# Where the first operand and seven weight blocks of the second output stage are prepared in a two-layer hybrid encoder kernel

## Chip, cores and metric

One core of one Trainium2 chip runs the whole program. The metric is the device time in microseconds (us) of one execution; for the kernel before it is the median of three runs.

## What is computed

The reference runs two layers over 2048 tokens of width 1024. Layer 0 has windowed attention, layer 1 dense latent attention with 16 heads; each is followed by the same kind of output stage. What matters here is layer 1:

```python
logits = (einsum('bqhd,bshd->bhqs', qn_b, k_nope) + einsum('bqhr,bsr->bhqs', qr_b, k_rope)) * scale
probs = softmax(logits, axis=-1)
o = einsum('bhqs,bshd->bqhd', probs, v)          # dense attention, 16 heads
y = (o * silu(z)) @ w_out                        # output stage, first product
h = h + y
gate = sigmoid(rms_norm(h, ple_norm_g) @ ple_w_gate)
h = h + (p @ ple_w) * gate
out = rms_norm(h, final_norm_g)
```

## The kernel before, in words

Every 32-bit factor is split into a high part (a cast to the fp32r type) and a low part (the difference), and a product is three matmuls (`mm3`, L290 to L292). The split of a block in SBUF is `split_sbuf`: ACT casts the high part (L216), and POOL or DVE subtracts (L218).

The program is a list of steps, each with a due time; `Plan.run` sorts them and writes the instructions of PE, ACT, DVE and POOL in that order, and each engine works its own list in order. The order of the DMA issues on SP is left to the scheduler. Due times in the dense attention count steps; in the output stages a time in us is multiplied by `US` = 1/1.3 to become steps.

**Dense attention** (`Dense`): 64 units (16 heads x 4 groups of 512 queries) of 16 steps, one step for 128 keys. A step `kt` of unit `u` issues on PE three score products (L1622 to L1624), one product of a coming unit whose row maximum is wanted (L1591, `max_step`), and two value products (L1654, L1655), which run 4.3 steps later. ACT does the exponential (L1626) and the cast to the high part (L1627). POOL subtracts for the low part (L1634). DVE reduces the maximum product (L1595, called the reduction below) and adds the probabilities to their sum in PSUM (L1644, the sum). The maximum products write to two PSUM banks in turn (`m_ps`), so one of them waits until the reduction of the one two before it is done. Once a unit, two products for the denominators (L1681, at 8.4 steps) and a transpose (L1607, at 9.6) take a turn in these same two banks, DVE splits the finished sum (L223), adds the two halves of the output (L1663) and folds the maxima (L1600). The maximum products run one to two units ahead, so the last 24 steps (from step 8 of unit 62) have none, and no reductions.

**Output stage** (`Post`, the second object, `final`): for the first 512 tokens `o_load` fetches a block of the attention output, its reciprocal denominators and its gate, `o_gate` multiplies them in two instructions (L768 and L769), and `o_cut` splits the result into the operand (L216, L218). Eight such blocks make the first operand. `w_load` and `w_split` do the same for a 1024 x 128 block of the weights (L703; L216 and L218 on 128x1024). `front` is one product of 24 matmuls over the eight operand blocks and one weight block. The operands of later token groups go through L757 (PE), L764 (DVE), L765 (POOL), L216 and L218.

`enter` turns the tables of `early_tables` into steps: a `w` entry is the due time of a split, with its load 4 us ahead; an `o` entry is the due time of the products, the distance to the split, the block, and which engines multiply. "dve" puts both products on DVE; "both" puts the first on POOL and the second on DVE. Times count from the start of the output stage, half a step after the end of the dense attention.

Of the kernel before, what the change touches and what calls it, by code (L numbers as in the profile page):

```python
# [73 lines left out]
GATES = [45, 55, 65, 126] + [(25 + i) * UNIT + 1 for i in range(4)]  # L74
E_W, E_O, E_P, E_M = (-16.54, -8.54, -0.54), -44.33, 4.77, ('mix', 'mix', 'mix', 'mix', 'mix', 'mix', 'mix', 'mix')
def early_tables():
    return (
    {
        "w": ([E_W[0], E_W[1], E_W[2], 5, 11, 17, 21, 25], GATES),
        "o": [(E_O + E_P * i, 2.5, i, E_M[i]) for i in range(8)],  # L80
        "renew": [(0.2, (("X", F32R), ("Y", F32R)))],
    },
    {
        "w": ([-4, 1, 5, 9, 13, 17, 21, 25], GATES),
        "o": [(-31 + 3.6 * i, 1.2, i, "dve") for i in range(8)],
        "renew": [(32 * UNIT + 1, (("Z", F32),))],
    },
)
# [1665 lines left out]
@with_exitstack  # L1754
def trunk(ctx, tc: tile.TileContext, a: dict, out):
    k = K(tc.nc, tc, a, ctx)
    rest = phase_a1(k)
    plan = Plan(k)
    end = phase_a2(k, plan, rest) + BASE[0]
    post = Post(k, 0, SPOTS[0], k.a_o, k.a_rden, k.a_z, a["a_w_out"][0], a["c_xT"], k.h1, 3)  # L1760
    end = post.enter(plan, end, early_tables()[0]) + BASE[1]
    end = Latents(k).schedule(plan, end) + BASE[2]
    dense = Dense(k)
    end = Gates(k).schedule(plan, end, dense) + BASE[3]
    end = dense.schedule(plan, end) + BASE[4]
    post = Post(k, 1, SPOTS[1], k.b_o, k.b_rden, k.b_z, a["b_w_out"][0], k.h1, out, 1)
    post.enter(plan, end, early_tables()[1])
    plan.run()
# [42 lines left out]
```

## Time and profile before

| | us |
|---|---|
| median of three runs | 3708.15 (3703.82 to 3709.5) |
| profiled execution | 3707.77 |
| its span in the trace | 3705.7 |
| PE busy | 3559.0 (96%) |
| DVE, ACT, POOL busy | 2400.5 (65%), 2277.3 (61%), 1969.9 (53%) |

A busy PE is not yet one at its own pace: matmuls overlap, and what counts is the distance from one start to the next. In the trace an engine's row tells start, duration, line, operation and tiles; a bracket at its end is the idle time ahead of it and what ended that. The stretches that matter are the dense attention (about 1760 to 3275 us of the span) and the first 100 us of the output stage behind it.

### The profile page before, as it was taken

The numbers are of one execution on the slowest core, as the hardware profiler recorded it, in microseconds if no ns is written. First come the engines' busy times: TensorE is split into PE (matmuls) and PEld (weight loads), VectorE is DVE, ScalarE is ACT, GpSimd is POOL, SyncE is SP. The second block draws the span as 40 slices with busy tenths as digits, with TensorE's granted clock in tenths as the row PEclk, the third lists the DMA queues.
The fourth block names the chain that finished last, engine by engine and source line by source line (L and its number), as shares of the span: only waits on it lengthen the run. The fifth ranks groups of instructions, "written<-read, shape, count | busy, mean of one in ns | idle before, by whom it ended". The sixth has DMA issues, their size and how long they took to land. (4 is left out here: it accounts for less than half of the span.)

```text
span 3705.7 us, 52399 instructions
## 1 busy us (share of the span) xinstructions
PE 3559.0 (96%) x17102; PEld 2971.5 (80%) x17102; DVE 2400.5 (65%) x4507; ACT 2277.3 (61%) x4267; POOL 1969.9 (53%) x1564
## 2 busy tenths in 40 slices
PE   6999999998999899999999999999999999989997
PEld 5788878886777799899888888888888888767776
DVE  5211149996444444523989898989898989964445
ACT  5211169995233443422989898989898989852333
POOL 3332120024324433110989898989898989953243
PEclk8999999999999999999999999999999999999998
DMA  6433278887754676654121212121212121166633
GB/s 169 129 119 111 75 204 203 200 193 204 168 151 131 175 203 204 220 190 136 26 58 35 58 35 58 35 58 36 56 35 55 38 63 35 31 192 170 172 98 106
DMA packets 384888, 429.25 MB, mean 116 GB/s; under 512 B 50579, under 2 KB 237459, under 8 KB 383910
## 3 DMA queue, kind: packets, MB, share of 16 engines
q1 hardware_dynamic: 365598, 391.81, 39.2%
q10 hardware_dynamic: 19016, 34.10, 2.6%
q8 instruction: 134, 2.20, 0.3%
q14 instruction: 140, 1.15, 0.1%
HBM read 252.71 MB, written 156.18 MB: 110 GB/s over the span
## 5 line engine op out<-in xcount | busy, mean ns | idle before, releaser
L1634 POOL TENSOR_TENSOR blkR<-blkF,blkX 128x512 fp32r<-128x512 f32 x1024 | 1351.0, 1331 | 180.3 <-PE ps L1624 51.3
L1595 DVE TENSOR_REDUCE blkF<-ps 128x1 f32<-128x512 f32 x1024 | 700.3, 684 | 79.2 <-PE ps L1591 43.8
L1626 ACT ACTIVATE blkF<-ps 128x512 f32<-128x512 f32 x1024 | 611.0, 597 | 101.1 <-PE ps L1624 60.8
L1627 ACT CAST blkX<-blkF 128x512 fp32r<-128x512 f32 x1024 | 635.4, 621 | 32.8
L1644 DVE TENSOR_TENSOR ps<-ps,blkF 128x512 f32<-128x512 f32 x896 | 615.4, 687 | 0.7
L1655 PE MATMUL ps<-blkR 128*128 128x512 f32 x1024 | 405.7, 396 | 1.1 <-POOL blkR L1634 1.1
L1654 PE MATMUL ps<-blkX,blkR 128*128 128x512 f32 x1024 | 405.7, 396 | 0.0
L290 PE MATMUL ps<-blkR 128*128 128x512 f32 (+2 forms) x888 | 342.9, 386 | 8.2 <-ACT blkR L216 8.2
L291 PE MATMUL ps<-blkR 128*128 128x512 f32 (+2 forms) x888 | 341.3, 384 | 1.2 <-DVE blkR L218 1.2
L292 PE MATMUL ps<-blkR 128*128 128x512 f32 (+2 forms) x888 | 340.9, 384 | 0.6 <-DVE blkR L218 0.6
L819 POOL TENSOR_TENSOR blkF<-blkF 128x512 f32<-128x512 f32 (+1 forms) x112 | 145.1, 1296 | 249.2 <-ACT blkF L813 239.1
L352 DVE TENSOR_TENSOR blkF<-ps,blkF 128x512 f32<-128x512 f32 x72 | 49.3, 691 | 329.8 <-PE ps L292 278.7
L218 POOL TENSOR_TENSOR blkR<-blkF,blkR 128x1024 fp32r<-128x1024 f32 (+1 forms) x39 | 73.4, 1885 | 306.1 <-ACT blkR L216 278.5
L1655 PEld LDWEIGHTS ps<-blkR 128*128 128x128 f32 x1024 | 195.0, 190 | 46.9 <-POOL blkR L1634 2.3
L1654 PEld LDWEIGHTS ps<-blkX,blkR 128*128 128x128 f32 x1024 | 195.0, 190 | 44.3
L813 ACT ACTIVATE blkF<-blkF 128x512 f32<-128x512 f32 (+1 forms) x120 | 72.2, 602 | 223.8 <-DVE blkF L798 114.4
L290 PEld LDWEIGHTS ps<-blkR 128*128 128x128 f32 x888 | 172.4, 194 | 40.5 <-ACT blkR L216 9.4
L292 PEld LDWEIGHTS ps<-blkR 128*128 128x128 f32 x888 | 171.6, 193 | 32.3 <-DVE blkR L218 1.2
L291 PEld LDWEIGHTS ps<-blkR 128*128 128x128 f32 x888 | 171.8, 193 | 31.1 <-DVE blkR L218 1.9
L223 DVE TENSOR_TENSOR blkR<-ps,blkR 128x512 fp32r<-128x512 f32 (+2 forms) x232 | 143.6, 625 | 52.3 <-ACT blkR L222 51.8
L290 PE MATMUL ps<-blkR,blkX 128*128 128x512 f32 (+1 forms) x384 | 150.4, 392 | 22.1 <-DVE blkF L352 13.8
L1622 PE MATMUL ps<-blkZ 96*128 96x512 f32 x384 | 155.6, 405 | 6.7 <-ACT blkF L1626 6.7
(268 smaller groups left out, 9021.2 us busy)
## 6 DMA issues: line engine op xcount, KB each, us to landing
h<-blkF SPq DMA_DIRECT2D x96, 256.0 KB
blkF<-h SPq DMA_DIRECT2D x80, 256.0 KB
a_qs<-blkF ACTq DMA_DIRECT2D x64, 256.0 KB
ple<-blkF SPq DMA_DIRECT2D x64, 256.0 KB
blkF<-h SPq DMA_DIRECT2D x32, 512.0 KB
b_v<-blkX SPq DMA_DIRECT2D x32, 512.0 KB
b_q<-blkX SPq DMA_DIRECT2D x64, 256.0 KB
blkZ<-b_q SPq DMA_DIRECT2D x64, 256.0 KB
```

What stands on the lines that cost most here:

```text
L290: mm(out, lhsT=lh, rhs=rh, start=(first and i == 0), stop=False)
L291: mm(out, lhsT=lh, rhs=rl, start=False, stop=False)
L292: mm(out, lhsT=ll, rhs=rh, start=False, stop=(last and i == n - 1))
L819: getattr(self.k.nc, eng).tensor_tensor(out=acc, in0=acc, in1=sq, op=ALU.add)
L1595: nc.vector.tensor_reduce(out=mm[:, qt, kc : kc + 1], in_=ps, axis=AX.X, op=ALU.max)
L1622: nc.tensor.matmul(sp, lhsT=kl[:, kt_], rhs=qh[0:96, :], start=True, stop=False)
L1626: nc.scalar.activation(pe, sp, AF.Exp, scale=SCALE_B)
L1627: nc.scalar.copy(ph, pe)
L1634: nc.gpsimd.tensor_tensor(out=pl, in0=pe, in1=fv(ph), op=ALU.subtract)
L1644: nc.vector.tensor_tensor(out=st["acc"], in0=prev, in1=st[kt][0], op=ALU.add)
L1654: nc.tensor.matmul(st["o"], lhsT=v, rhs=ph, start=(kt == 0), stop=False)
L1655: nc.tensor.matmul(st["o"], lhsT=v, rhs=pl, start=False, stop=(kt == NT - 1))
```

## The change

One table is changed, that of the second output stage. The eight operand blocks, prepared from 31 us ahead of the stage in distances of 3.6 us by DVE alone, are now due at -200, -181, -163, -145, -127, -110, -92 and -33 us, with the first product on POOL and the split 2.6 us behind the products instead of 1.2. Of the eight weight blocks, due from -4 to 25 us before, seven are now due at -190, -173, -153, -137, -68, -55 and -43 us, and the eighth at 13.

```diff
     {
-        "w": ([-4, 1, 5, 9, 13, 17, 21, 25], GATES),
-        "o": [(-31 + 3.6 * i, 1.2, i, "dve") for i in range(8)],
+        "w": ([-190, -173, -153, -137, -68, -55, -43, 13], GATES),
+        "o": [(t, 2.6, i, "both") for i, t in enumerate((-200, -181, -163, -145, -127, -110, -92, -33))],
         "renew": [(32 * UNIT + 1, (("Z", F32),))],
     },
```

In steps, operand blocks 0 to 7 come at unit 54 step 6, unit 55 step 5, unit 56 step 3, unit 57 steps 0 and 14, unit 58 step 11, unit 59 step 9 and unit 62 step 7. Weight blocks 0 to 6 come at unit 54 step 14, unit 55 step 11, unit 56 step 10, unit 57 step 7, unit 60 step 12 and unit 61 steps 6 and 15. The list of PE is the same in both kernels.

On DVE, in unit 54, the rows around steps 5 to 8 were these before (reduction and sum in turn, then the fold):

```order
L1644 TENSOR_TENSOR ps<-ps,blkF 128x512
L1595 TENSOR_REDUCE blkF<-ps 128x1
L1644 TENSOR_TENSOR ps<-ps,blkF 128x512
L1595 TENSOR_REDUCE blkF<-ps 128x1
L1644 TENSOR_TENSOR ps<-ps,blkF 128x512
L1600 TENSOR_REDUCE blkF<-blkF 128x4
```

and are these now:

```order
L1644 TENSOR_TENSOR ps<-ps,blkF 128x512
L769 TENSOR_TENSOR blkF<-blkF 128x512
L1595 TENSOR_REDUCE blkF<-ps 128x1
L1644 TENSOR_TENSOR ps<-ps,blkF 128x512
L1595 TENSOR_REDUCE blkF<-ps 128x1
L1644 TENSOR_TENSOR ps<-ps,blkF 128x512
L1600 TENSOR_REDUCE blkF<-blkF 128x4
L218 TENSOR_TENSOR blkR<-blkF,blkR 128x512
```

The second product of block 0 (L769) stands ahead of the reduction of step 7, and the subtraction of its split (L218) behind that of step 8.

On POOL, whose list holds the low parts of all 1024 steps (L1634), this stood from the start of the dense attention to that of the output stage:

```order
L1545 MEMSET blkR 1x2048
L1634 TENSOR_TENSOR blkR<-blkF,blkX 128x512 x1024
L731 TENSOR_TENSOR blkR<-ident 128x1024
L733 MEMSET blkR 128x512 x2
L819 TENSOR_TENSOR blkF<-blkF 128x512
```

and this stands there now, with the first products (L768) of the first three blocks:

```order
L1545 MEMSET blkR 1x2048
L1634 TENSOR_TENSOR blkR<-blkF,blkX 128x512 x871
L768 TENSOR_TENSOR blkF<-blkF 128x512
L1634 TENSOR_TENSOR blkR<-blkF,blkX 128x512 x14
L768 TENSOR_TENSOR blkF<-blkF 128x512
L1634 TENSOR_TENSOR blkR<-blkF,blkX 128x512 x14
L768 TENSOR_TENSOR blkF<-blkF 128x512
```

Eight products have come into POOL's list; the first stands behind the low part of step 6 of unit 54.

On DVE, in unit 62 behind the last reduction, this stood before, the first two of eight groups:

```order
L1600 TENSOR_REDUCE blkF<-blkF 128x4
L768 TENSOR_TENSOR blkF<-blkF 128x512
L769 TENSOR_TENSOR blkF<-blkF 128x512
L1644 TENSOR_TENSOR ps<-ps,blkF 128x512
L218 TENSOR_TENSOR blkR<-blkF,blkR 128x512
L1644 TENSOR_TENSOR ps<-ps,blkF 128x512 x2
L768 TENSOR_TENSOR blkF<-blkF 128x512
L769 TENSOR_TENSOR blkF<-blkF 128x512
```

and this stands there now, block 7 with it:

```order
L769 TENSOR_TENSOR blkF<-blkF 128x512
L1595 TENSOR_REDUCE blkF<-ps 128x1
L1644 TENSOR_TENSOR ps<-ps,blkF 128x512 x2
L1600 TENSOR_REDUCE blkF<-blkF 128x4
L218 TENSOR_TENSOR blkR<-blkF,blkR 128x512
L1644 TENSOR_TENSOR ps<-ps,blkF 128x512 x5
```

Seven of the eight groups have left the last 24 steps.

## Rows read from the trace of the kernel before

**Rows 1.** Busy time by stretch: us; PE, PEld, DVE, ACT, POOL (count); clock; DMA share, GB/s.

```profile
3080.00:3174.00 94.00, 94.00 (x407) 76.06 (x406) 85.77 (x145) 85.03 (x148) 85.95 (x67) 1.00 0.13 35
3174.00:3268.00 94.00, 88.27 (x362) 69.23 (x361) 87.61 (x130) 80.71 (x141) 82.73 (x60) 0.96 0.24 66
```

**Rows 2.** Timeline of PE, one steady unit: start, duration, line; step 7, step 8, denominators.

```profile
3093.04 0.40 PE L1591 MATMUL ps<-blkR,blkZ 96*128 96x512 f32 x1
...
3094.44 0.40 PE L1591 MATMUL ps<-blkR,blkZ 96*128 96x512 f32 x1
...
3095.13 0.62 PE L1681 MATMUL ps<-blkE,ones 128*128 128x512 f32 x2
```

**Rows 3.** Timeline of DVE in the same unit: reductions of steps 6, 7 and 9.

```profile
3092.64 0.68 DVE L1595 TENSOR_REDUCE blkF<-ps 128x1 f32<-128x512 f32 x1
...
3093.84 0.68 DVE L1595 TENSOR_REDUCE blkF<-ps 128x1 f32<-128x512 f32 x1
...
3096.72 0.69 DVE L1595 TENSOR_REDUCE blkF<-ps 128x1 f32<-128x512 f32 x1 [0.34 <-PE ps L1591]
```

**Rows 4.** Timeline of ACT in the same unit: the cast of step 6.

```profile
3092.52 0.62 ACT L1627 CAST blkX<-blkF 128x512 fp32r<-128x512 f32 x1
```

**Rows 5.** Timeline of POOL in the same unit: seven low parts, then that of step 9.

```profile
3087.84 9.45 POOL L1634 TENSOR_TENSOR blkR<-blkF,blkX 128x512 fp32r<-128x512 f32 x7 [0.34 <-PE ps L1591]
...
3097.86 1.30 POOL L1634 TENSOR_TENSOR blkR<-blkF,blkX 128x512 fp32r<-128x512 f32 x1 [0.56 <-ACT blkX L1627]
```

**Rows 6.** Line 769: instructions, duration in ns (min/median/max), first and last start.

```profile
L769 DVE TENSOR_TENSOR blkF<-blkF x8: 1635/1662/1673, 3234.4 to 3272.5; 128x512 f32<-128x512 f32 x8
```

**Rows 7.** Timeline of DVE: a split beside POOL's low parts; a weight block's.

```profile
3236.78 1.02 DVE L218 TENSOR_TENSOR blkR<-blkF,blkR 128x512 fp32r<-128x512 f32 x1
...
3276.95 1.45 DVE L218 TENSOR_TENSOR blkR<-blkF,blkR 128x1024 fp32r<-128x1024 f32 x1 [0.65 <-ACT blkR L216]
```

**Rows 8.** Timeline of DVE in the output stage: a 128x4 product.

```profile
3359.19 1.21 DVE L246 TENSOR_TENSOR blkF<-blkF 128x4 f32<-128x4 f32 x1
```

**Rows 9.** Timeline of POOL at the same time, and at the dense end.

```profile
3278.14 2.65 POOL L1634 TENSOR_TENSOR blkR<-blkF,blkX 128x512 fp32r<-128x512 f32 x2 [0.82 <-ACT blkX L1627]
...
3359.09 1.29 POOL L765 TENSOR_TENSOR blkF<-blkF 128x512 f32<-128x512 f32 x1
```

**Rows 10.** Timeline of PE at the end of the dense attention; brackets: idle ahead, its end.

```profile
3230.84 0.40 PE L1591 MATMUL ps<-blkZ 96*128 96x512 f32 x1
...
3231.53 0.40 PE L1622 MATMUL ps<-blkZ 96*128 96x512 f32 x1
...
3242.86 0.50 PE L1622 MATMUL ps<-blkZ 96*128 96x512 f32 x1 [1.20 <-ACT blkF L1626]
...
3253.67 0.79 PE L1622 MATMUL ps<-blkZ 96*128 96x512 f32 x1 [2.80 <-ACT blkF L1626]
...
3260.24 0.44 PE L1622 MATMUL ps<-blkZ 96*128 96x512 f32 x1
...
3276.97 0.50 PE L290 MATMUL ps<-blkR 128*128 128x512 f32 x1 [2.80 <-ACT blkR L216]
...
3287.64 0.39 PE L290 MATMUL ps<-blkR 128*128 128x512 f32 x1
```

**Rows 11.** Timeline of ACT at the dense end.

```profile
3236.13 0.62 ACT L216 CAST blkR<-blkF 128x512 fp32r<-128x512 f32 x1 [0.78 <-DVE blkF L769]
```

**Rows 12.** Timeline of DVE in the first product of the output stage.

```profile
3314.58 1.21 DVE L218 TENSOR_TENSOR blkR<-blkF,blkR 128x1024 fp32r<-128x1024 f32 x1
3315.72 0.68 DVE L764 TENSOR_TENSOR blkF<-ps,blkF 128x512 f32<-128x512 f32 x1
```

**Rows 13.** Timeline of PE there, and an isolated wait in the latent projections.

```profile
1274.19 0.42 PE L290 MATMUL ps<-blkZ,blkR 128*128 128x336 f32 x1 [2.12 <-ACT blkR L216]
1274.45 0.32 PE L291 MATMUL ps<-blkZ,blkR 128*128 128x336 f32 x1
...
3334.63 0.50 PE L291 MATMUL ps<-blkZ,blkR 128*128 128x512 f32 x1 [0.62 <-DVE blkZ L218]
```

## Prediction

> **What bounds the kernel now.** I read the busy time by stretch first. In a steady stretch of the dense attention PE is busy for all 94.00 us, DVE for 85.77, ACT for 85.03, POOL for 85.95 [rows 1]. PE sets the pace: six products a step, 1.40 us from one maximum product to the next, 0.233 us each [rows 2]. Whatever stops PE here is lost in full. The other three have some 8 us to spare in 94, about 2.0 us in a unit of 23 us. In the stretch that holds the end, PE falls to 88.27 of 94 and the clock to 0.96 [rows 1].
>
> Then the timeline of PE at that end. The last maximum product is at 3230.84, and step 8 of unit 62 starts at 3231.53; from there on PE needs five products a step. It stops again and again for ACT's exponential: 1.20, 2.80 us, and 2.80 us for the cast of the first weight block; after the stop at 3253.67 the next 15 products take until 3260.24, 6.57 us where 3.50 would do, at the lower level of the clock, 1.2 GHz [rows 10]. The cause stands in ACT's timeline: the cast of an operand block waits for the second product on DVE [rows 11], and the exponentials are queued behind that cast. So preparing the eight blocks late does cost time; the second weight product begins at 3287.64 [rows 10].
>
> **What the end gives back.** Seven operand blocks and the weight waits leave this stretch. PE's own pace would be 24 steps x 5 x 0.233 = 28 us, but POOL needs 24 low parts x 1.325 us (two in 2.65, [rows 9]) = 31.8 us, so POOL is late next. A cast ends 1.5 us after its step's maximum product (step 6: product at 3091.64, one step ahead of [rows 2]; cast until 3093.14, [rows 4]). Step 8's low part can so start at 3230.84 + 1.40 + 1.5 = 3233.7, and the last ends at 3265.5. Block 7 still lies here: its first product on POOL adds 1.3 us, and twice POOL stands aside for DVE for 0.6 us (a DVE instruction every 0.60, [rows 3]): 3268.0. In PE's list the first weight product stands ahead of the last three steps' value products, so it can start three low parts earlier, at 3264.0, plus 0.6 for the values of the step before: 3264.6. Its 24 products and six value products, at 0.233, end at 3271.6. Before, the second weight product began at 3287.64: 16.0 us gained. Block 7 also delays the reductions (next part, 3.1 us, of which 2.5 are counted): 0.6 less. In the first product of the stage, a weight split of 1.21 us stood on DVE ahead of an operand block's first step [rows 12], and PE later stops for the last of these blocks [rows 13]: about 1.1 us more. Sum 16.5. Bounds: 12.5 if POOL comes to this stretch 4 us late, 19 if block 7 costs nothing.
>
> **What ten units have to bear.** Block 0, in the steady unit of the rows, where step 7's maximum product is at 3093.04. POOL reaches the first product behind the low part of step 6. The cast ends at 3093.14 [rows 4], the low part at about 3094.5, the product at 3095.85 (2 x 1.33). POOL has no lead there: it waits for ACT's cast at 3097.86 [rows 5]. DVE has done the reduction of step 6 (3092.64) and the sum, and is free at 3093.84, where its next reduction stood [rows 3]. Now L769 is there and waits for POOL until 3095.85: 2.0 us.
>
> L769 is not seen in this place. In the last 24 steps it took 1.66 us each of eight times [rows 6], more than two times 0.60. A 128x4 product on DVE took 1.21 us and ended, at 3360.40, just as a POOL instruction ended [rows 8, 9]: a DVE product of two SBUF tiles can wait for the POOL instruction that runs. So L769 costs between 0.60 and 1.66 us, by whether POOL's next low part, ready by then, starts first. DVE is free again at 3096.45 or 3097.5, and the reduction of step 7 ends 0.7 later, at 3097.1 or 3098.2. PE's denominator product, at 3095.13 [rows 2], takes that reduction's bank: PE stops 2.0 or 3.1 us. The split of 1.02 us [rows 7] comes two steps later on a DVE that is still behind: 0.45 more. Block 0 costs 2.5 or 3.55 us. Behind the waiting L769 stand reductions and sums; PE waits for the reductions, ACT (four exponentials of buffer) not yet.
>
> The Trainium skill, "SBUF — State Buffer", "SBUF: two separate sides", says that GpSimd and a DVE instruction with two SBUF inputs share one port pair as an exclusive lock: whichever starts first holds it for its whole instruction. [rows 6] agree; by it alone both ends of L769's price stay open.
>
> The same working for blocks 1 to 6 at their steps (5, 3, 0, 14, 11, 9), where a reduction two steps on takes the place of the denominators, gives 3.35, 3.85, 4.55, 3.7, 3.1 and 2.9 us with the long L769; block 3 is the dearest, since splitting the sum, adding the output halves and a weight split follow within six steps. Sum of seven 25.0; with the short L769 1 us less each, 18. No row decides which of the two starts first, so I take the middle, 21.5. The seven weight splits cost DVE 1.45 us each [rows 7] in units with 2.0 to spare; only block 5's, ahead of a denominator product, is charged: 0.5. ACT's 0.62 per operand and about 1.05 per weight block, 11.7 us in all, are hidden by its spare time and three score banks; without that cover they would be added. POOL's eight products are hidden where PE stops longer than they take, as here. The loads (five transfers for a block, one for a weight) go past the row stores and query loads on SP in stretches with the DMA engines at 0.13 [rows 1]: nothing, unless SP holds up the maxima's row, which has over five steps in hand.
>
> The clock: after waits of 1.2, 0.2, 1.2 and 2.8 us it fell, at 3.1 us for 15 products [rows 10]; an isolated wait of 2.12 us was followed by products at the usual 0.32 [rows 13]. I charge one fall in seven stops: 3.
>
> Total on the profiled execution, 3707.8 (0.4 below the median, which changes nothing): 3707.8 + 21.5 + 0.5 + 3 - 16.5 = 3716.3. Forecast **3716 us**. A block that stops PE by less than (16.5 - 0.5) / 7 = 2.3 us turns the sign.
>
> **Rivals.** (1) *No wait for POOL, faster.* If POOL runs ahead, or DVE comes late anyway, L769 finds its input ready. A block then costs DVE 0.60 + 1.02, with a weight 3.1, against 2.0 spare a unit and over 1 us that a reduction may be late: 2 us in all. 3707.8 - 16.5 + 2 = 3693. It decides once L769's input is ready within 0.5 us of DVE's coming. [rows 5] speak against it, since POOL waits for ACT. (2) *L769 always short, no clock fall*: 3707.8 + 18.5 - 16.5 = 3710, no difference. (3) *L769 always long*: 3707.8 + 25.5 + 3 - 16.5 = 3720. POOL's next low part is ready before its product ends, and eight rows of eight are long [rows 6]. The Trainium skill, "Perfetto Trace Analysis", "Optimizing Scalar/DVE Operations", warns that moving work between GPSIMD and DVE may not help, as they share a read port; that is this rival. (4) *The clock falls at each stop*: 7 x 3 instead of 3, 3734; one row speaks for it, one against [rows 10, 13]. (5) *The end is not shortened as the change says*, POOL arriving late: gain 12.5, 3720; it lies in the forecast's range.
>
> **How the numbers follow.** Measuring tells 0.2% (7.4 us) from no change, so slower begins at 3715.5. Forecast with its spread (3708 to 3724, rival 5 in it) 0.45, of which 0.27 slower and 0.18 same; rival 1 0.20, faster; rival 2 0.15, same; rival 3 0.12 and rival 4 0.08, slower. Faster 0.20, same 0.33, slower 0.47. The range leaves out most of rival 4 and the better half of rival 1: 3693 to 3728.
>
> **What would show it.** In the trace after: PE stops in units 54 to 59, once or twice a block, released by DVE's reduction or sum; DVE idle 1.5 to 2.6 us ahead of L769 for POOL; L769 at 0.6 or 1.66 us; those units 25 to 27 us long; no stops for ACT in the last 24 steps, which take about 33 us, and the first weight product without a wait. I am wrong if PE stays at its pace through units 54 to 61 (rival 1), if the clock falls there (rival 4), or if PE still stops for casts at the end.

## The result: slower by 0.9%, more than forecast

The changed kernel took 3739.96 us (median of four runs, 3738.38 to 3743.77); the kernel before took 3706.78 (median of four). The ratio is 1.0093 (95% interval 1.0078 to 1.0108): slower, as forecast, but by 33 us instead of 8, and outside the range. The profiled execution took 3738.38 us, with a span of 3736.6. PE, DVE, ACT and POOL are TensorE, VectorE, ScalarE and GpSimd; the expectations below use the longer names.

The two stretches that answer to [rows 1], in the same columns (busy time of PE, PEld, DVE, ACT, POOL, then the clock):

```profile
3080.00:3174.00 94.00, 83.88 (x320) 64.28 (x321) 81.15 (x126) 71.07 (x122) 70.47 (x54) 0.91 0.26 76
3174.00:3268.00 94.00, 84.74 (x344) 65.79 (x343) 80.14 (x127) 75.09 (x129) 76.29 (x58) 0.96 0.17 48
```

PE was busy for all 94 us of the first stretch and now loses 10 of them, and every other engine is less busy than before: all of them wait for each other in turn. The timeline of PE shows where it stops (the bracket is the idle time and what ended it). From the top: blocks 0 and 1, weight blocks 3, 4 and 5, block 7, and then the first two weight products of the output stage:

```profile
3049.55 1.22 PE L1681 MATMUL ps<-blkE,ones 128*128 128x512 f32 x2 [4.30 <-DVE blkF L1595]
...
3080.00 0.80 PE L1591 MATMUL ps<-blkR,blkZ 96*128 96x512 f32 x1 [4.61 <-DVE blkF L1595]
...
3142.37 0.50 PE L1681 MATMUL ps<-blkE,ones 128*128 128x512 f32 x1 [2.33 <-DVE blkF L1595]
...
3232.11 0.50 PE L1591 MATMUL ps<-blkZ 96*128 96x512 f32 x1 [1.64 <-DVE blkF L1595]
...
3249.76 0.50 PE L1591 MATMUL ps<-blkZ 96*128 96x512 f32 x1 [1.85 <-DVE blkF L1595]
...
3283.42 0.37 PE L1607 MATMUL ps<-ident,blkF 128*4 128x128 f32 x1 [6.08 <-DVE blkF L1600]
...
3312.31 0.39 PE L290 MATMUL ps<-blkR 128*128 128x512 f32 x1
...
3319.15 0.39 PE L290 MATMUL ps<-blkR 128*128 128x512 f32 x1
```

Each of these stops ends with a reduction or a fold on DVE. The last two rows answer to [rows 10]: the first weight product no longer waits for anything.

What holds DVE is in its own timeline and in POOL's. DVE, the second product of blocks 0, 1, 2 and 7:

```profile
3045.94 2.96 DVE L769 TENSOR_TENSOR blkF<-blkF 128x512 f32<-128x512 f32 x1 [2.06 <-POOL blkF L768]
...
3074.55 4.20 DVE L769 TENSOR_TENSOR blkF<-blkF 128x512 f32<-128x512 f32 x1 [1.36 <-POOL blkF L768]
...
3103.18 1.74 DVE L769 TENSOR_TENSOR blkF<-blkF 128x512 f32<-128x512 f32 x1 [2.42 <-POOL blkF L768]
...
3277.10 4.19 DVE L769 TENSOR_TENSOR blkF<-blkF 128x512 f32<-128x512 f32 x1 [2.06 <-POOL blkF L768]
```

POOL beside blocks 0 and 1 (x2 and x3: so many low parts back to back, without idle time):

```profile
3044.64 1.27 POOL L768 TENSOR_TENSOR blkF<-blkF 128x512 f32<-128x512 f32 x1
3045.88 2.47 POOL L1634 TENSOR_TENSOR blkR<-blkF,blkX 128x512 fp32r<-128x512 f32 x2
...
3073.23 1.28 POOL L768 TENSOR_TENSOR blkF<-blkF 128x512 f32<-128x512 f32 x1
3074.48 3.72 POOL L1634 TENSOR_TENSOR blkR<-blkF,blkX 128x512 fp32r<-128x512 f32 x3
```

L769 first waits for POOL's product (2.06 us at block 0), and then it is not 1.66 us long as in [rows 6] but 2.96 beside two low parts and 4.20 beside three: it ends half a microsecond after POOL's run of low parts has ended. At the weight blocks DVE waits for ACT instead. Here is block 4, DVE and then ACT:

```profile
3229.98 1.47 DVE L218 TENSOR_TENSOR blkR<-blkF,blkR 128x1024 fp32r<-128x1024 f32 x1 [2.16 <-ACT blkR L216]
```

```profile
3228.90 1.05 ACT L216 CAST blkR<-blkF 128x1024 fp32r<-128x1024 f32 x1
```

DVE stood still for 2.16 us, since its subtraction comes next in its list while the cast stands behind exponentials in ACT's.

For the comparisons below I add up, from the rows of PE, the idle time in brackets, and separately what the distances between starts exceed 0.233 us per product (mostly products at the lower clock; column "slow"). "Middle" is units 53 to 62, up to the last maximum product, "end" what follows up to the first weight products of the stage. Each row is read from one trace. The ratios are each against runs of the kernel before on the same chip in the same session (its median was 3718, 3692, 3693 and 3704 us in the four sessions, each of which had another chip):

| kernel | middle: idle + slow | end: idle + slow | sum | ratio (95%) |
|---|---|---|---|---|
| before | 0 + 0 | 11.2 + 8.2 | 19.4 | 1 |
| changed | 28.5 + 17.4 | 6.1 + 2.4 | 54.4 | 1.0093 (1.0078 to 1.0108) |
| no_second | 20.4 + 15.7 | 2.2 + 2.0 | 40.3 | 1.0062 (1.0042 to 1.0082) |
| wait_no_lock | 20.9 + 16.3 | 2.6 + 3.3 | 43.1 | 1.0074 (1.0054 to 1.0094) |
| no_first | 11.8 + 11.3 | 1.7 + 0.4 | 25.2 | 1.0022 (1.0008 to 1.0035) |
| weights_early | 6.8 + 5.0 | 7.6 + 6.9 | 26.3 | 1.0024 (1.0014 to 1.0034) |
| early_dve | 21.5 + 16.4 | 5.3 + 2.8 | 46.0 | 1.0055 (1.0042 to 1.0069) |
| early_pool | 25.0 + 14.1 | 2.4 + 2.6 | 44.1 | 1.0054 (1.0039 to 1.007) |
| weights_apart | 7.5 + 7.8 | 8.2 + 5.8 | 29.3 | 1.002 (1.0011 to 1.0029) |
| combo | 5.0 + 5.4 | 7.2 + 6.2 | 23.8 | 1.0019 (1.001 to 1.0028) |
| operands_pool | 16.1 + 10.7 | 2.7 + 2.2 | 31.7 | 1.0032 (1.0019 to 1.0044) |
| weights_pool | 13.9 + 9.4 | 5.7 + 7.9 | 36.9 | 1.0061 (1.0047 to 1.0074) |
| one_source | 8.0 + 7.0 | 2.5 + 0.5 | 18.0 | 0.9999 (0.999 to 1.0008) |
| three_apart | 0 + 0 | 5.8 + 5.7 | 11.5 | 0.998 (0.9971 to 0.9989) |
| five_apart | 5.3 + 2.5 | 4.9 + 3.6 | 16.3 | 0.9995 (0.9986 to 1.0004) |

The sum accounts for the time of the changed kernel: 54.4 - 19.4 = 35 us against 33 measured. For the others it comes within 4 us of what the ratio gives, but for early_dve (26.6 against 20), early_pool (24.7 against 20) and weights_pool (17.5 against 23), so differences of a few us between rows should not be read closely. (Expectations that give 57.8 or 50.4 us for the changed kernel were worked out over a longer stretch or counted the stop of 4.30 us twice.)

### The profile page after: what moved, and what is told of

The parts are those of the page before. It is cut to its first block, busy times and chain, and to the rows that moved or that the text cites. A ratio compares the mean times of both kernels' runs of the same rounds, so it can differ in the third digit from the quotient of the medians.

```text
span 3736.6 us, 52404 instructions
## 1 busy us (share of the span) xinstructions
PE 3576.1 (96%) x17102; PEld 2980.9 (80%) x17102; DVE 2401.3 (64%) x4499; ACT 2276.5 (61%) x4267; POOL 1976.0 (53%) x1572
## 5 line engine op out<-in xcount | busy, mean ns | idle before, releaser
L1634 POOL TENSOR_TENSOR blkR<-blkF,blkX 128x512 fp32r<-128x512 f32 x1024 | 1347.4, 1327 | 213.4 <-PE ps L1624 71.3
L1654 PE MATMUL ps<-blkX,blkR 128*128 128x512 f32 x1024 | 407.6, 398 | 0.0
L218 POOL TENSOR_TENSOR blkR<-blkF,blkR 128x1024 fp32r<-128x1024 f32 (+1 forms) x39 | 73.4, 1886 | 303.7 <-ACT blkR L216 276.2
L1654 PEld LDWEIGHTS ps<-blkX,blkR 128*128 128x128 f32 x1024 | 196.3, 192 | 43.9
```

What stands on the lines that cost most here:

```text
L1634: nc.gpsimd.tensor_tensor(out=pl, in0=pe, in1=fv(ph), op=ALU.subtract)
L1654: nc.tensor.matmul(st["o"], lhsT=v, rhs=ph, start=(kt == 0), stop=False)
```

## Experiments

**First theory: the hand-over and L769.** The first runs took L769 for the whole cause (theory A), its wait alone (A2), or the added load (B).

no_second leaves L769 out for the eight blocks; their operands lack a factor.

```diff
-        two.tensor_tensor(out=of, in0=of, in1=rt, op=ALU.mult)
+        if not self.final:
+            two.tensor_tensor(out=of, in0=of, in1=rt, op=ALU.mult)
```

> The changed kernel without the second product of the eight operand blocks (L769 on DVE), so the first operand stays without its gate; POOL's first product, the splits and the weight blocks stay where they are. Theory A (hand-over and lock): the stops of PE come from L769, which waits 1.4 to 2.4 us for POOL and then is kept from its two SBUF inputs for 1.7 to 4.2 us; then nearly all of the 28 us of waits at the operand blocks go, and with them most of the 18 us at the low clock: 3698 to 3704 us. Theory B (load): it is the added work itself, eight products on POOL and fifteen splits on DVE and ACT, that PE pays for: above 3722 us.

Theory A fell: the ratio was 1.0062, and 36 of 46 us in the middle stayed. On the scale of the expectations that is 3730 us, as theory B had it, so B was still open here. What stood at the stops was new. DVE, POOL and PE at block 0 (reduction L1596, low part L1635, maximum product L1592 in this kernel):

```profile
3060.04 4.50 DVE L218 TENSOR_TENSOR blkR<-blkF,blkR 128x512 fp32r<-128x512 f32 x1 [0.58 <-ACT blkR L216]
```

```profile
3059.02 4.97 POOL L1635 TENSOR_TENSOR blkR<-blkF,blkX 128x512 fp32r<-128x512 f32 x4
```

```profile
3065.20 0.79 PE L1592 MATMUL ps<-blkR,blkZ 96*128 96x512 f32 x1 [4.17 <-DVE blkF L1596]
```

The split's subtraction, 0.69 us long behind block 0 in the changed kernel, had taken over the role of L769: 4.50 us beside four low parts at block 0 (the first of them nearly over), and 5.37 us beside four at block 1. It does not read what POOL writes, so this isn't a wait for a result. Both instructions read two tiles in SBUF.

wait_no_lock puts a reduction with one source in L769's place, which still waits for POOL's product; no_first leaves out POOL's product L768. In both, the operands lack a factor.

```diff
-        two.tensor_tensor(out=of, in0=of, in1=rt, op=ALU.mult)
+        if self.final:
+            nc.vector.tensor_reduce(out=rt[:, 0:1], in_=rt, axis=AX.X, op=ALU.max)
+        else:
+            two.tensor_tensor(out=of, in0=of, in1=rt, op=ALU.mult)
```

> The changed kernel with L769 replaced, for the eight operand blocks, by a DVE reduction of the first product's result: it waits for POOL in the same place but reads one SBUF tile, not two; the first operand stays without its gate. Theory A: DVE still waits about 2 us, but the instruction takes 0.7 us instead of 1.74 to 4.20 (20.0 us for the eight), so some 14 us of waits and a part of the low clock go: 3715 to 3724 us, and PE still stops at each block, by 1 to 2 us. Theory A2 (the wait for POOL alone is the price, the length of L769 only hides in it): 3734 to 3741 us.

```diff
-        one.tensor_tensor(out=rt, in0=rt, in1=zt, op=ALU.mult)
+        if not self.final:
+            one.tensor_tensor(out=rt, in0=rt, in1=zt, op=ALU.mult)
```

> The changed kernel without the first product of the eight operand blocks (L768 on POOL); L769 stays on DVE and multiplies with the reciprocal alone. DVE then waits for nothing but its own two SBUF inputs. Theory A: L769 still takes 1.2 to 4 us beside POOL's low parts, the wait of 2 us is gone: 3712 to 3724 us. Theory A2 (the wait alone): L769 near 0.7 us and 3698 to 3704 us.

The reductions in L769's place took 0.69 us each; but the hand-over (a wait of 1.37 to 2.42 us for POOL's product) and the split's subtraction, up to 2.48 us now, kept 37 us in the middle. The ratio of 1.0074 is 3734 us on the scale of the expectations, which is the number of A2, the wait alone; no_second, where DVE had no such wait and lost as much, speaks against A2 as the whole cause. Without POOL's product the middle fell to 23 us, though DVE kept both its instructions (L769's 0.70 to 1.78 us). So POOL's one product per block makes half of the cost, by DVE's wait for it and by the low parts that it makes late; no_first takes away both at once and doesn't part them.

weights_early moves the weight blocks alone.

```diff
-        "w": ([-4, 1, 5, 9, 13, 17, 21, 25], GATES),
+        "w": ([-190, -173, -153, -137, -68, -55, -43, 13], GATES),
```

> The kernel before with the new due times of the weight blocks alone; the operand blocks are prepared over the last 24 steps by DVE, as before. Theory A: the splits in the units 54 to 61 cost PE at most what they cost in the changed kernel (0.24, 0.24, 0.24, 2.33, 1.64, 1.85, 0.24 us), and the wait of 2.8 us for the first weight block's cast with its 0.6 us and the low clock behind it goes: 3701 to 3707 us. Theory B: 3710 us or more.

The weights alone cost more in the middle (11.8 us) than they give at the end (4.9): ratio 1.0024, again what theory B had named.

**Second theory (A'):** any DVE instruction with both sources in SBUF is kept out while POOL works through a queue that has fallen behind, and one product more puts the queue behind. early_dve and early_pool move the products, and in early_pool also the cast and the subtraction, to one engine.

```diff
-        "o": [(t, 2.6, i, "both") for i, t in enumerate((-200, -181, -163, -145, -127, -110, -92, -33))],
+        "o": [(t, 2.6, i, "dve") for i, t in enumerate((-200, -181, -163, -145, -127, -110, -92, -33))],
```

> Both products of the eight operand blocks on VectorE (as in the kernel before), everything else as in the changed kernel. What no_second showed: with the second product left out, it is the operand split's subtraction (line 218, both sources in SBUF) that is long, 4.50 and 5.37 us beside four and five low parts that GpSimd runs back to back, its queue being one product late. Theory A' (any VectorE instruction with both sources in SBUF is kept out until GpSimd's queue has run dry, and it is GpSimd's extra product, 1.28 us, that keeps the queue from running dry): VectorE's three instructions of a block are short again, none over 2 us, although VectorE has 0.68 us more to do per block; lost time from unit 53 to the second stage's first product (TensorE idle plus its excess at the lower clock: 23.8 us before, 57.8 after, 28.6 without GpSimd's product) 32 to 40 us, ratio 1.002 to 1.004. Theory B (VectorE has no room for the added work, whoever shares it): more work on VectorE than in the changed kernel, so no better than it, 57 us or more, ratio 1.009 or more.

```diff
+        "o": [(t, 2.6, i, "pool") for i, t in enumerate((-200, -181, -163, -145, -127, -110, -92, -33))],
```

> The whole preparation of the eight operand blocks (two products, the cast, the subtraction) on GpSimd, everything else as in the changed kernel: VectorE and ScalarE have no part in it. Theory A': no VectorE instruction with both sources in SBUF is left at the operand blocks, so the stops with a wait for the reduction go there and only those at the weight blocks stay; GpSimd falls 4 x 1.28 = 5.1 us behind at each block, and if a low part then comes too late TensorE waits for GpSimd's low part, not for VectorE: lost time 28 to 45 us, ratio 1.000 to 1.006. Theory C (GpSimd's load, whatever VectorE does, is what slows the stage): four times the added GpSimd work, so well above the changed kernel's 57.8 us, ratio over 1.012.

early_dve missed both expectations (46 us, between 40 and 57): three instructions per block, 16 of the 24 between 1.4 and 1.8 us (one of 3.91), are too many, as probe_dve explains below. early_pool came out at the upper end of what A' had named (44 us, 1.0054), and it showed the mechanism most clearly. DVE has nothing to do at the operand blocks, so POOL's late queue met a weight block's subtraction. DVE, POOL, PE:

```profile
3047.54 7.41 DVE L218 TENSOR_TENSOR blkR<-blkF,blkR 128x1024 fp32r<-128x1024 f32 x1 [0.21 <-ACT blkR L216]
```

```profile
3042.69 11.18 POOL L1634 TENSOR_TENSOR blkR<-blkF,blkX 128x512 fp32r<-128x512 f32 x9
```

```profile
3055.61 0.80 PE L1591 MATMUL ps<-blkR,blkZ 96*128 96x512 f32 x1 [6.18 <-DVE blkF L1595]
```

An instruction of 1.45 us [rows 7] took 7.41, and PE stopped for 6.18.

weights_apart is weights_early with the subtraction two steps behind the cast; combo adds that distance for the operand blocks, at their old times.

```diff
-                tables += [(t - PS_WL, "w_load", (n, f)), (t, "w_split", (n, f))]
...
+                    tables += [(t, "w_cast", (n, f)), (t + 2.6, "w_low", (n, f))]
```

> As weights_early (the kernel before with the new weight times alone; ratio 1.0024), but the subtraction of a weight block on VectorE is due 2.6 steps after the cast on ScalarE, where both stood at one due time. Theory W (the stop at a weight block is VectorE waiting for the cast, which stands behind two to three exponentials and casts in ScalarE's queue; 2.16, 1.40 and 1.04 us of waiting at blocks 4, 5 and 3 in the changed kernel): the TensorE stops of 2.39, 1.64 and 1.84 us go or fall under 0.5 us, and with them their slow products; lost time 18 to 23 us against 29.6 of weights_early and 23.8 of the kernel before; ratio 0.998 to 1.000. Rival L (the 1.4 us of the subtraction itself is what VectorE has no room for): nothing changes, ratio 1.002 to 1.003.

```diff
-        "o": [(-31 + 3.6 * i, 1.2, i, "dve") for i in range(8)],
+        "o": [(-31 + 3.6 * i, 2.6, i, "dve") for i in range(8)],
```

> weights_apart, and in addition the split of the operand blocks 2.6 steps after their products, where the kernel before has 1.2, at the old times. Theory E (TensorE's waits for exponentials in the last two units, 1.20, 1.20, 2.80 and 1.18 us in the kernel before, come from ScalarE's cast of an operand block standing in its queue until the second product has ended): these waits shrink to under 1 us in sum, the lost time falls by another 6 to 12 us below weights_apart, ratio 0.995 to 0.998. Rival (ScalarE or VectorE is simply full in these units): the waits stay, same ratio as weights_apart.

DVE's waits for the cast went, as theory W said, yet the time did not: ratio 1.002, the number of rival L, though it comes about otherwise. Stops of 1.74, 1.58, 1.44 and 1.41 us came up at other places. DVE and POOL at the first (first sum L1658, low part L1648 here):

```profile
3079.16 3.64 DVE L1658 TENSOR_TENSOR ps<-blkF 128x512 f32<-128x512 f32 x1
```

```profile
3078.46 5.46 POOL L1648 TENSOR_TENSOR blkR<-blkF,blkX 128x512 fp32r<-128x512 f32 x4
```

This is the first sum of a unit, which adds two probability tiles in SBUF (`ps<-blkF`); the other fourteen read PSUM and one tile (`ps<-ps,blkF`) and are never over 0.70 us in the units at hand. In the kernel before, the first sums of ten units from 3000 to 3240 us were short, all of them (duration in ns, min/median/max):

```profile
L1644 DVE TENSOR_TENSOR ps<-blkF x10: 690/692/692, 3016.2 to 3225.7; 128x512 f32<-128x512 f32 x10
```

So the steady units already hold one exposed instruction each. In the kernel before it was never held off: POOL's low part beside it took 1.85 us there instead of 1.25. Where POOL was shifted against DVE, as here, some of these sums were held off; that the shift does it is argued, not tried by itself. combo's extra distance at the end gave back nothing that the ratio shows (1.0019): theory E fell; the waits for exponentials only changed places.

**Probes.** Two kernels add work on a scratch tile to the kernel before, mostly one addition per unit: probe_dve on DVE alone, probe_pool on POOL alone. Each ran once, so only their traces are read.

```diff
...
+            if kind == "max":
+                nc.vector.tensor_reduce(out=zt[:, 0:1], in_=of, axis=AX.X, op=ALU.max)
+            else:
+                eng = nc.vector if kind == "dve" else nc.gpsimd
+                eng.tensor_tensor(out=zt, in0=of, in1=rt, op=ALU.mult)
```

> The kernel before with eight additions on VectorE alone, one per unit, on a scratch tile (nothing of the output depends on them): at step 9 of units 54 to 57 one, two, three and four maximum reductions of a 128x512 tile in SBUF (one source, about 0.6 us each); at step 9 of unit 58 one, of unit 59 two and of unit 61 three products of two SBUF tiles, at step 3 of unit 60 one. Theory A' with a slack S (VectorE may fall about 1.2 us behind before TensorE stops, read from the changed kernel, where a weight block's 1.4 us without a wait stopped TensorE 0.24 us): stops of 0, at most 0.3, 0.6 to 0.9 and 1.2 to 1.5 us for the four reductions' groups; the single products 0.7 to 1.9 us long with stops of 0 to 0.7. Rival L (VectorE has no room at all): every addition stops TensorE by its whole length, 0.6, 1.2, 1.8, 2.4. Rival P (only the port matters): no stop at the reductions at all.

DVE's additions at step 9 that led to a stop were four reductions, and two and three products (DVE; reduction L723, product L726):

```profile
3114.84 2.84 DVE L723 TENSOR_REDUCE blkF<-blkF 128x1 f32<-128x512 f32 x4
...
3161.70 3.48 DVE L726 TENSOR_TENSOR blkF<-blkF 128x512 f32<-128x512 f32 x2
...
3210.54 5.16 DVE L726 TENSOR_TENSOR blkF<-blkF 128x512 f32<-128x512 f32 x3
```

The stops of PE that followed:

```profile
3118.34 0.50 PE L1611 MATMUL ps<-blkR,blkZ 96*128 96x512 f32 x1 [0.65 <-DVE blkF L1615]
...
3165.84 0.50 PE L1611 MATMUL ps<-blkZ 96*128 96x512 f32 x1 [1.30 <-DVE blkF L1615]
...
3216.35 0.80 PE L1611 MATMUL ps<-blkZ 96*128 96x512 f32 x1 [2.97 <-DVE blkF L1615]
```

Length less stop is 2.19, 2.18 and 2.19 us: at step 9 an addition to DVE may last 2.19 us, and each microsecond beyond that stops PE for as long. One, two and three reductions (0.68, 1.40, 2.12 us) and one product (1.78) did not stop it. My slack of 1.2 us was too small for this step; at step 3 it is less (a product of 1.84 us, stop 0.94, so 0.9). The theory's form held, rivals L and P fell. Here, where POOL is not late, a product takes 1.64 to 1.84 us instead of 0.68: it lets one low part pass.

> The kernel before with eight additions on GpSimd alone, a product of two SBUF tiles of 128x512 (1.28 us) on a scratch tile; VectorE gets nothing to do. One product at step 9 of unit 54 and two at step 9 of unit 58 (the middle of a unit); one product 3.3, 2.3 and 1.3 steps before the first sum of units 56, 57 and 58 and again 3.3 before that of unit 62, two products 3.3 steps before that of unit 60; one right after the first sum of unit 61. (The first sum of a unit, line 1644 with both sources in SBUF, is the only regular VectorE instruction of this kind; it takes 0.69 us in the kernel before.) Theory A': the first sums that follow a late GpSimd queue take 1.9 to 5 us, and TensorE stops there for 0.8 to 4 us with a wait for the reduction; in the middle of a unit nothing happens, VectorE having no such instruction there. Rival B (it is VectorE's added load that stops TensorE): no stop at VectorE anywhere, since VectorE has no more to do than before.

This was wrong in most places. A single product on POOL cost nothing anywhere: the first sums behind it took 0.69 to 1.46 us, and there was no stop; nor did two at step 15 stop PE. But two products in the middle of unit 58, where I had expected nothing, left POOL so late that it met the first sum of unit 59, some eight steps on. POOL, DVE, PE (low part L1654, first sum L1664; the second and third row of POOL overlap, and belong to one run of eleven low parts that ends at 3152.28):

```profile
3135.89 2.66 POOL L726 TENSOR_TENSOR blkF<-blkF 128x512 f32<-128x512 f32 x2
3138.52 6.29 POOL L1654 TENSOR_TENSOR blkR<-blkF,blkX 128x512 fp32r<-128x512 f32 x5
...
3142.28 10.00 POOL L1654 TENSOR_TENSOR blkR<-blkF,blkX 128x512 fp32r<-128x512 f32 x8
```

```profile
3147.61 5.22 DVE L1664 TENSOR_TENSOR ps<-blkF 128x512 f32<-128x512 f32 x1
```

```profile
3153.48 0.80 PE L1611 MATMUL ps<-blkZ 96*128 96x512 f32 x1 [3.32 <-DVE blkF L1615]
```

DVE had not one instruction more than before, so rival B fell here: two short products on POOL, 12 us earlier, stopped PE for 3.32 us. But a late POOL need not do this. At the first sum of unit 59 the low part in progress had started 1.4 us after its cast had ended; at that of unit 60, behind two more products, some 2.5 us after, and this sum took only 1.29 us.

**The load against the second source.** one_source is the changed kernel with L769 and the split's subtraction replaced by reductions over one tile.

```diff
-        two.tensor_tensor(out=of, in0=of, in1=rt, op=ALU.mult)
...
+            nc.vector.tensor_reduce(out=of[:, 0:1], in_=of, axis=AX.X, op=ALU.max)
...
-            k.split_sbuf(of, hi, lo, pool_lo=(how == "mix"))
...
+                nc.scalar.copy(hi, of)
+                nc.vector.tensor_reduce(out=lo[:, 0:1], in_=fv(hi), axis=AX.X, op=ALU.max)
```

> The changed kernel with VectorE's two instructions per operand block (second product, line 769; subtraction of the split, line 218) replaced by maximum reductions over one tile of the same 128x512, which read one source in SBUF and don't wait for GpSimd's product. The number of instructions on every engine, GpSimd's product and the weight blocks stay as in the changed kernel; the output is not the reference's, since blocks are left without second product and low half. Theory A' (two sources in SBUF, beside a late GpSimd queue): none of the replaced instructions is over 0.75 us, no stop at the operand blocks beyond 0.3 us; what is left is the weight blocks (6.8 us idle and 5 us at the lower clock up to the last maximum product in weights_early) and first sums; lost time up to the last maximum product 10 to 18 us where the changed kernel had 50.4 and wait_no_lock, in which the subtraction kept its two sources, 37.2; ratio 1.001 to 1.003. Rival B (VectorE's added load): the same two instructions of 0.6 us are still there, so at least two thirds of the 50 us stay, ratio over 1.006.

With the same number of instructions on every engine the 33 us are gone: 0.9999, even below what A' had expected. The replaced lines (ns, min/median/max):

```profile
L770 DVE TENSOR_REDUCE blkF<-blkF x8: 666/672/680, 3044.7 to 3244.4; 128x1 f32<-128x512 f32 x8
...
L784 DVE TENSOR_REDUCE blkR<-blkR x8: 669/686/687, 3047.9 to 3248.2; 128x1 fp32r<-128x512 f32 x8
```

The weight blocks' stops stay (2.33, 1.64, 1.84 us), so at least the operand blocks' cost is settled: it is the second SBUF source and the wait for POOL's product, not the number of instructions. The reductions wait for nothing on POOL, so this run alone doesn't part the two. PE's stops at the seven early operand blocks, added up, do it in part: 21.7 us in the changed kernel, 14.4 in wait_no_lock (the wait is kept, and the subtraction's two sources), 13.6 in no_second (no wait on DVE for POOL, the subtraction's two sources), 4.8 in no_first (both instructions with two sources, without POOL's product) and 1.2 here. Either of the two alone costs much of the whole, and they don't add up.

**Versions made from this.** operands_pool and weights_pool put most of the early work on POOL, in pieces.

```diff
+        if i == 0:
+            nc.vector.tensor_tensor(out=rt, in0=rt, in1=zt, op=ALU.mult)
+        elif i == 1:
+            nc.gpsimd.tensor_tensor(out=of, in0=of, in1=rt, op=ALU.mult)
+        elif i == 2:
+            nc.scalar.copy(hi, of)
+        else:
+            nc.gpsimd.tensor_tensor(out=lo, in0=of, in1=fv(hi), op=ALU.subtract)
```

> The kernel before with operand blocks 0 to 6 made ready early, one per unit 54 to 60, in four pieces apart from each other: the first product on VectorE at step 9, the second on GpSimd at step 12.5, the cast on ScalarE at step 15, the subtraction on GpSimd at step 6.5 of the next unit; block 7 as before, 3.9 us later. The weight blocks stay late. So VectorE has one short instruction per block instead of three, and GpSimd 2.56 us per unit in the places where it stood idle (1.3 us at step 5 and 1.5 us at step 13 of a unit before). Theory A': one product on VectorE costs at most 0.3 us of stop, the first sums stay under 1.5 us; lost time up to the last maximum product 0 to 8 us (0 before, 50 in the changed kernel), the end 12 to 16 us shorter than before; ratio 0.996 to 0.999. Theory C (GpSimd has no room for 2.56 us per unit, it falls behind by the unit and holds the first sums): lost time 20 us or more in the middle, ratio 1.001 or more.

```diff
+        c = slice(4 * i - 4, 4 * i)
+        k.nc.gpsimd.tensor_tensor(out=lo[:, c], in0=src[:, c], in1=fv(hi[:, c]), op=ALU.subtract)
```

> The kernel before with seven weight blocks of the second output stage early (units 55 to 63), the cast on ScalarE, the subtraction in two halves of 128x512 on GpSimd at steps 6.5 and 13, nothing on VectorE; operands as before. Theory A': without VectorE's 1.4 us and its wait for the cast (up to 2.2 us) the stops of weights_early (6.8 us of idle, 5.0 us at the lower clock up to the last maximum product) go, unless the second half makes a first sum late; lost time there 0 to 4 us, ratio 0.998 to 1.000 where weights_early had 1.0024. Theory C (GpSimd has no room): first sums of 2 us and more in most of these units, ratio 1.002 or more.

Both went as theory C has it, 1.0032 and 1.0061. In operands_pool the one product that DVE keeps per block took, at step 9:

```profile
L776 DVE TENSOR_TENSOR blkF<-blkF x7: 1729/4843/6320, 3041.5 to 3202.3; 128x512 f32<-128x512 f32 x7
```

The stops fit the measured slack: 4.85 - 2.19 = 2.66 us, which PE shows four times within 0.02, and 6.32 - 2.19 = 4.13, seen once. In weights_pool the first sums took 3.36 us in the median.

three_apart keeps POOL out of it and gives DVE one instruction per unit, at step 9; five_apart has blocks 0 to 4 early, with the second product on POOL (there block 6 is loaded over what block 4 still needs; the work is the same).

```diff
-        "o": [(-31 + 3.6 * i, 1.2, i, "dve") for i in range(8)],
+        "o": [(-31 + 5.2 * i, 2.6, i + 3, "dve") for i in range(5)],
...
+        for c, times in {0: [(54, 9), (55, 9), (56, 7), (56, 9)], 1: [(57, 9), (58, 9), (59, 7), (59, 9)], 2: [(60, 9), (61, 9), (62, 7), (62, 9)]}.items() if self.final else ():
+            for i, (u, s) in enumerate(times):
+                t = (16 * (u - 64) + s) * 1.3
...
+                tables.append((t, "o_part", (c, i)))
```

> The kernel before with operand blocks 0 to 2 early, wholly on VectorE (cast on ScalarE), one VectorE instruction per unit, at step 9 of units 54 to 62, and the other five blocks in the last two units, 5.2 apart instead of 3.6; weights as before; nothing on GpSimd. From probe_dve, where single two-source products at step 9 took 1.78 us and stopped TensorE not at all: no stop up to the last maximum product over 0.3 us, lost time there 0 to 3 us; at the end five blocks instead of eight, 4 to 8 us less than before; ratio 0.998 to 0.9995. Rival: the one instruction per unit adds up (VectorE has some 2 us per unit to spare, 8.2 of 94 us idle in four units), stops appear from the third unit on, ratio 1.001 or more.

> As three_apart, but blocks 0 to 4 early, two units each: the first product on VectorE at step 9, the second on GpSimd at step 12.5, the subtraction on VectorE at step 9 of the next unit; three blocks late. VectorE has one instruction per unit, GpSimd one product of 1.28 us every other unit, which probe_pool showed to cost nothing alone. If the two costs don't meet: lost time up to the last maximum product 0 to 4 us, the end 8 to 12 us shorter, ratio 0.997 to 0.9985. Rival (they meet: GpSimd still late at step 9 of the next unit, VectorE's subtraction 3 us and longer, as in operands_pool, where GpSimd had two per unit): stops of 2.6 us at every other unit, ratio 1.001 or more.

three_apart is the one version faster than both kernels, and it came as expected: 3695.66 us against 3704.26, ratio 0.998 (0.9971 to 0.9989). Busy time in two stretches, as in [rows 1], and the first products (ns):

```profile
3040.00:3134.00 94.00, 94.00 (x407) 76.05 (x406) 89.28 (x149) 85.65 (x150) 86.78 (x67) 1.00 0.17 47
3134.00:3228.00 94.00, 94.00 (x407) 76.04 (x406) 89.28 (x149) 85.65 (x149) 86.96 (x67) 1.00 0.12 31
```

```profile
L776 DVE TENSOR_TENSOR blkF<-blkF x3: 1779/1781/1781, 3047.4 to 3185.2; 128x512 f32<-128x512 f32 x3
```

DVE is busier than in the changed kernel, 89.28 us against 81.15, and PE never stops here. In five_apart a single product of POOL at step 12.5, in a unit where DVE had a product at step 9, was enough, each of four times, to make the next first sum 3.2 us long and stop PE for 1.30 to 1.33 us:

```profile
L1665 DVE TENSOR_TENSOR ps<-blkF x7: 690/3204/3231, 3059.3 to 3203.4; 128x512 f32<-128x512 f32 x7
```

The end became 10.9 us shorter and the middle 7.8 us longer; what is left can't be told from no change.

## Where the prediction was right and wrong

The direction and the place of the cost were right, the size was wrong, by these terms:

- **The wait for POOL's product** was forecast at 2.0 us for block 0 and 1.5 to 2.6 in general; it was 2.06 and 1.36 to 2.43. Right.
- **L769 at 0.60 to 1.66 us** was wrong. Five of eight took 1.74, the others 2.96, 4.20 and 4.19. The step that failed is "a DVE product of two SBUF tiles can wait for the POOL instruction that runs": it can wait for several. The bound of 1.66 came from eight places that all let DVE in after one low part. The rule of the Trainium skill, "SBUF — State Buffer", "SBUF: two separate sides", that whichever starts first holds the shared ports for its whole instruction, agrees with the 1.78 us products, which let one low part pass; the 4.20 us beside three low parts it does not give.
- **Seven operand blocks, 21.5 us**: PE's stops there sum to 21.7 (4.30, 4.61, 2.96, 2.17, 2.17, 2.82, 2.71). That the sum fits is luck, since its parts do not: blocks 0 and 1 cost more than either end (L769), blocks 3 and 4 less than either, because at their steps DVE may be later than I counted (2.19 us at step 9).
- **Weight splits, 0.5 us**: 6.8 measured (2.33, 1.64, 1.85 and four times 0.24). I charged the 1.45 us of the subtraction and called ACT's cast hidden; but DVE stands still until the cast is done, up to 2.16 us, with its reductions behind it.
- **The clock, 3 us**: 17.4 measured, the largest miss, and with it a sign came true that the prediction had named for being wrong: the granted clock fell in these units, to 0.91 in the first stretch. Rival 4, a fall at every stop, comes nearest the result (3734 forecast), but it was not at every stop. In the changed kernel the products behind the stops of 4.30 and 4.61 us took some 3 us too long, behind those of 2.96, 1.85 and 1.64 us 1.8 each, behind two of 2.17 us 1.9 and 1.7, but behind the third of 2.17 and those of 2.33 and 2.07 us 0.3 or less; behind four stops of 1.3 us in five_apart 0.5 to 0.7. The rows of before already had it: at the end 11.2 us of idle time came with 8.2 of slow products, and I charged one of seven stops.
- **The end, 16.5 us back**: from the last maximum product to the second weight product it was 56.80 us and became 45.45, so 11.4. Block 7 is the difference: 0.6 us forecast, 6.08 of stop and about 2.2 of slow products measured, for the same reason as blocks 0 and 1. Without it the end would have given 19.6, and the wait of the first weight product is gone, as forecast. In the first product behind it 0.8 us came back of 1.1.

With the measured terms the sum is 3716.3 + 0.2 + 6.3 + 14.4 + 4.4 = 3742 us (the end with its 0.8), against 3738.38 for the profiled execution, whose dense attention happened to begin 4.2 us earlier than in the trace of before. Rival 1 (no wait) is refuted by the rows above. Rival 3 (L769 always long) had its sign, but the seven blocks cost 21.7 us and not its 25.5; of the 25 us that the sum missed, the clock has 14.4.

What stays open: which rule lets POOL go several times in a row. DVE was kept out for two to six low parts only where POOL had fallen behind, since only then is the next low part ready when one ends. But this is not enough. At block 2 of the changed kernel POOL had three low parts without idle time, as at block 1, and the cast of the second had ended before L769 began, as at block 0. POOL at block 2, then ACT's casts of the second low part at blocks 0 and 2:

```profile
3103.11 4.18 POOL L1634 TENSOR_TENSOR blkR<-blkF,blkX 128x512 fp32r<-128x512 f32 x3
```

```profile
3045.27 0.62 ACT L1627 CAST blkX<-blkF 128x512 fp32r<-128x512 f32 x1
...
3102.42 0.62 ACT L1627 CAST blkX<-blkF 128x512 fp32r<-128x512 f32 x1
```

At block 0 L769 was kept out for both low parts (2.96 us); at block 2 it was let in after one (1.74 us), and POOL's three took 4.18 us instead of 3.72. So a late POOL tells where DVE may be held off for long, not that it will be. Nor was a version tried that moves more than three blocks without POOL; DVE has 4.7 of 94 us left in three_apart.

## What to carry over

An engine that is off the critical path can still make another one's instructions longer: before work is added to GpSimd, look for VectorE instructions beside it that read two tiles in SBUF, count how far GpSimd's queue is behind there, and take the whole run of GpSimd instructions as the upper end of their price, not their own length; the lower end is one GpSimd instruction or less. Put such work where the waiting engine has slack and one piece at a time (here one VectorE instruction per unit at step 9 cost nothing, three in a row 3 us), and put nothing in its list whose input another engine's queue delivers late. To each microsecond of stop in an otherwise full TensorE stream add half to all of another for the clock, as these runs do.

## What the runs showed of the hardware that I had not expected

- A VectorE product of two SBUF tiles (128x512) took 0.68 us where no low part held it off, up to 1.84 where it let one pass, and 2.96 to 6.32 where GpSimd, being behind, ran two to five in a row first; a 128x1024 subtraction took up to 7.41. In the same units VectorE's reductions and sums that read PSUM, or a single SBUF tile, never took over 0.70 us.
- GpSimd's run of low parts shows afterwards which case it was: 1.24 to 1.25 us each (3 in 3.72, 8 in 10.00) while VectorE is kept out, and some 0.5 to 0.6 us more for a turn that VectorE gets in between (3 in 4.18 at block 2, 7 in 9.45 us in [rows 5]). GpSimd being behind is needed for the first case, but does not decide for it.
- The slack between two engines was constant to 0.01 us at one step: three additions of different kinds and lengths at step 9 gave 2.19, 2.18 and 2.19 us.
- The same kernel differed by 0.7% between sessions, each on another chip (medians of the kernel before, 3692 to 3718 us), more than most effects here; the runs don't part the chip from the session.
